# One more pair of the up projection as a seven-product step, and another rotation of PSUM banks beside it

## The chip, the core and the metric

One NeuronCore of a Trainium2 chip. TensorE (PE) multiplies, VectorE (DVE), ScalarE (ACT) and GpSimd (POOL) work on tiles, and DMAs are started from the queues of SyncE (SP), POOL and ACT. Each engine works through its own queue in order. The metric is the time of the whole kernel on the device in microseconds (us); lower is better.

## The reference

A residual block on x of 512 tokens by 1024 features, in float32. The change concerns the second half of it, the channel mixer:

```
h  = rms_norm(x, norm_ffn_g)
up = causal_dwconv(h @ w_up, conv_ffn_w)      # 1024 -> 2 * 2816, then 3 taps along the tokens
a, b = split(up, 2)
x  = x + (silu(a) * b) @ w_down               # 2816 -> 1024
```

Ahead of it stand a mixing layer (a gated short convolution and attention with forget gates) and behind it a last RMSNorm.

## The kernel before

**Layout and number format.** Features lie on partitions in blocks of 128, tokens along the free axis. Each float32 product is made of three matmuls: an operand is split into a rounded part ("h", as in `wh`, `x1h`, `gh`) and the rest ("l", as in `wl`, `x1l`, `gl`), and h·h, l·h and h·l are added up in PSUM. Weights come from DRAM in chunks (`raw_*`), in the order of the list `stream`. `split` makes a chunk's `wh` on ACT (L275) and its `wl` on DVE (L279, which needs `wh`). Two buffers each of `wh` and `wl` are used in turn, so a chunk can be split once PE has done with the chunk two places earlier.

**The up projection.** The 22 pairs j of 128 columns of a and of b are made in two phases, 0 to 11 and 12 to 21, and each phase is followed by down steps over what it made. There are two ways to make a pair:

- plain: two chunks of 1024 columns (`up12`, `up13` for pair 6), each summed over eight feature blocks in one PSUM bank (L309, and L327 for the first two blocks). Then DVE multiplies the bank by `rb2` into a tile `fz` (L1171), and three taps make `fu` (ACT L566, DVE L567 and L570).
- as a seven-product step (function `seven`): two by two blocks are multiplied with seven products in place of eight (Strassen-Winograd). A pair is two doubles, and each double comes as a chunk P of 768 and a chunk F of 1024 columns (`P18`, `F18`, `P19`, `F19`), multiplied at L327 into four banks at once, named `dn`. The function `merge` then puts the four banks together (ACT L1192; DVE L1193, L1197, L1201, L1202, L1206, and L1214 for `rb2`), and the same taps follow. The sums of weights that the F chunks need are made in DRAM by DMAs that add (`make_forms`: SP's L208, POOL's L211) while earlier stages run.

`SUP` names the pairs made in seven-product steps. Behind each pair `glu` applies SiLU on ACT (L1232) and multiplies a by b on POOL (`ge` L1235, `go` L1244). After each second pair, sums for the down steps (DVE L1253, L1254, L1257, L1258) and splits of the results (ACT L1262, DVE L1263, tile `gl`) follow.

**What sets the order.** PE runs the chunks in the order written. Work on ACT and DVE that need not be done at once goes into the list `later`, and `run_later` takes some of it after each split, up to an allowance in us:

```python
if any(("e",) in w[2] for w in later):
    run_later(k, {"u": 4.2, "P": 1.6, "F": 1.2}[nm[0]])
```

A merge puts nine items there. While one is waiting, the `fz` and the taps of the plain pairs behind it are queued up there too. Whoever takes a PSUM bank first calls `flush` with its number, which puts out all that stands in `later` up to the item that reads this bank. The plain pairs of phase 0 take their banks from the list `acc`, two a pair; seven-product steps take four, by `USETS`, in the order (products 2 and 3, products 4 and 5, products 1 and 6, product 7). The banks 6, 7, 0, 1 of pair 5 are so read at L1197, at L1202 and L1206, at L1192 and L1193, and at L1201. A scheduler then orders each engine's instructions; the tables below show the outcome.

Of the kernel before, what the change touches and what calls it, by code (L numbers as in the profile page):

```python
# [57 lines left out]
PLAIN = [(m, k) for m in (6, 7) for k in range(*PHASES[1])]  # L58
PCUTS = (0, 8, 12, 20)

SUP = ((1, 2, 5), (14, 17))
XF = (26, 0)
UPD = tuple(tuple(((j, q), (j, q + 1)) for j in js for q in (0, 2)) for js in SUP)
DOUBLES = GATES + UPD[0] + STEPS[0] + UPD[1] + STEPS[1]
# [6 lines left out]
def block_kernel(ctx, tc, xT, vecs, wv, win, wmix, wo, wup, wst, wdp, outT):  # L71
# [10 lines left out]
    def keep(ins):  # L82
        return tc.keep_in_program_order(ins)

    def bank(i, name):
        return ps.tile([P, S], F32, tag=f"b{i}", name=name)

    def ring(*ids):
        st = [0]

        def f(name):
            st[0] += 1
            return bank(ids[(st[0] - 1) % len(ids)], name)

        return f
# [33 lines left out]
    def step_chunks(n):  # L129
        m = len(DOUBLES[n])  # L130
        return [(f"P{n}", wst[n, :, : 3 * m * P], 3 * m * P), (f"F{n}", n, 4 * m * P)]
# [10 lines left out]
    for ph, (j0, j1) in enumerate(PHASES):  # L142
        for j in range(j0, j1):
            if j in SUP[ph]:
                stream += step_chunks(n) + step_chunks(n + 1)
# [72 lines left out]
    def slot():  # L218

        while todo_bg and todo_bg[0][0] <= make_forms.slot:  # L220
            todo_bg.pop(0)[1]()
        make_forms.slot += 1
# [14 lines left out]
    def flush(banks=None):  # L237

        def wanted(w):
            return set(w[2]) & set(banks) if banks is not None else True  # L240

        while any(map(wanted, later)):
            n = next(n for n, w in enumerate(later) if banks is None or wanted(w) or w[0] < len(parts))
            with after_split():
                later.pop(n)[3]()
# [501 lines left out]
    acc, bank_s, bank_t = ring(2, 0, 1), ring(3, 4), ring(5, 6)  # L747
# [76 lines left out]
    def seven(doubles, n0, sets, operand, done=None, of="q", tick=False):  # L824


        todo, wants = [], {}
        for n, d in enumerate(doubles):
            for kind in "PF":
                prods = []  # L830
                for s_, (i, q) in enumerate(d):
                    for f, g, b, h in PROD:
                        if (f < 3) == (kind == "P"):
                            wants.setdefault(f"{kind}{n0 + n}", []).append((of, q))
                            c = 3 * s_ + f if f < 3 else s_ + len(d) * (f - 3)
                            prods.append((c, i, operand(q, g), b, h))
                todo.append((f"{kind}{n0 + n}", prods))
        users = [{(i, b) for _, i, _, b, _ in prods} for _, prods in todo]
        for n, (name, prods) in enumerate(todo):
            if tick and name[0] == "P":  # L840
                slot()
            wh, wl = chunk(name)
            flush(wants[name])
            before = set().union(*users[:n])
            after = set().union(*users[n + 1 :])
            out = []
            for c, i, (xh, xl), b, h in prods:
                if i not in open_:
                    flush(sets[i])
                    open_[i] = [bank(x, f"dn{n0}{i}{x}") for x in sets[i]]  # L850
                cs = slice(c * P, (c + 1) * P)
                out.append((
                    open_[i][b][:, th[h]], (i, b), wh[:, cs], wl[:, cs], xh, xl,
                    (i, b) not in before, (i, b) not in after,
                ))
            passes(out, len(out))
            if name[0] == "F":
                for i in sorted({i for _, i, *_ in prods}):
                    if (i, 0) not in after:
                        done(i, open_.pop(i), sets[i])  # L860
            split_next()


    acc = ring(3, 4, 5, 6, 2, 7)
# [94 lines left out]
    for j in range(KB):  # L959
# [13 lines left out]
        else:  # L973
            if j == GJ:
                acc = ring(3, 4, 2, 7)
# [31 lines left out]
    acc = ring(0, 1, 5, 6, 3, 4, 2, 7)  # L1007
# [83 lines left out]
    def up_form(ph, q, g):  # L1091
        if g < 3:
            kb, hs = (2 * q, 2 * q + 1, 2 * q + 1)[g], th[(0, 0, 1)[g]]
            return x1h[:, kb, hs], x1l[:, kb, hs]
        n = XF[ph] + 4 * q + (0, 3, 1, 2)[g - 3]
        return gh[:, n, :], gl[:, n, :]
# [27 lines left out]
    def turns(*ids):  # L1124
        st = list(ids)

        def f(name):
            f.last = st.pop(0)
            flush((f.last,))
            return bank(f.last, name)  # L1130

        return f

    acc = turns(0, 1, *(2, 3, 4, 5) * 2, 6, 7, 0, 1, 2, 3, 4, 5)
    USETS = dict.fromkeys(SUP[1], (2, 3, 4, 5)) | {1: (2, 3, 4, 5), 2: (6, 7, 0, 1), 5: (6, 7, 0, 1)}
    ssq3 = xp.tile([P, S], F32, tag="ssq", name="ssq3")

    def place(ph, q):
# [2 lines left out]
    def up(j, ph, rb2, pu=None):  # L1141
# [6 lines left out]

        if j in SUP[ph]:
            c = 2 * SUP[ph].index(j)  # L1150
            slot()
            seven(
                UPD[ph][c : c + 2], NU[ph] + c, {j: USETS[j]}, lambda q, g: up_form(ph, q, g), of="x",
                done=lambda i, banks, ids: merge(ph, j, banks, ids, rb2, tap, uu),
# [27 lines left out]
    def merge(ph, j, banks, ids, rb2, tap, uu):  # L1182

        p23, p45, p16, p7 = banks[0], banks[1], banks[2], banks[3][:, th[0]]
        t, gs = {}, []

        def tile_of(nm):
            return fp.tile([P, S], F32, tag="fz", name=f"{nm}{j}", bufs=4)

        def z1():  # L1190
            t["z"] = tile_of("uz")
            nc.scalar.activation(t["z"][:, th[0]], p16[:, th[0]], AF.Copy)  # L1192
            nc.vector.tensor_add(t["z"][:, th[1]], p16[:, th[1]], t["z"][:, th[0]])  # L1193

        def m1():
            gs.append(tile_of("ua"))
            nc.vector.tensor_add(gs[0], p23, t["z"])  # L1197

        def u3():
            t["u"] = tile_of("uu")[:, : 2 * P]  # L1200
            nc.vector.tensor_add(t["u"], p7, t["z"][:, th[1]])  # L1201
            nc.vector.tensor_add(gs[0][:, th[1]], p45[:, th[1]], gs[0][:, th[1]])  # L1202

        def m2():
            gs.append(tile_of("ub"))
            nc.vector.tensor_add(  # L1206
                gs[1].rearrange(halves_of, h=2), p45.rearrange(halves_of, h=2),
                t["u"].unsqueeze(1).to_broadcast([P, 2, 2 * P]),
            )

        def fin(n):
            def f():
                g = gs[n]
                nc.vector.scalar_tensor_tensor(g, g, (1.0, -1.0)[n], rb2, op0=ALU.mult, op1=ALU.mult)  # L1214

            return f

        ev = ("e",)
        for f, us, x in (
            (z1, 0.42, 2), (m1, 0.7, 0), (u3, 0.85, 3), (m2, 0.7, 1),  # L1220
            (fin(0), 0.7, None), (lambda: tap(0, gs[0]), 1.4, None),
            (fin(1), 0.7, None), (lambda: tap(1, gs[1]), 1.4, None),
            (lambda: glu(ph, j, uu), 0, None),
        ):
            later.append((0, us, (ev,) if x is None else (ev, ids[x]), f))

    def glu(ph, j, uu):
# [11 lines left out]
        def sums():  # L1239
# [3 lines left out]
            def mul(eng):  # L1243
                return eng.tensor_mul(go[:, 0:2, :], a.rearrange(halves_of, h=2), b.rearrange(halves_of, h=2))  # L1244
            if j + 1 < PHASES[ph][1]:
                keep(mul(nc.vector if ph and j + 1 in SUP[ph] else nc.gpsimd))
            else:
# [80 lines left out]
    for ph, (j0, j1) in enumerate(PHASES):  # L1328
        if ph:
            acc = turns(*(6, 7, 0, 1) * 4)  # L1330
# [211 lines left out]
```

## Time and profile before

| | |
|---|---|
| median of 3 runs | 691.76 us (691.45 to 691.80) |
| the profiled execution, its own time | 692.09 us |
| its span, first to last instruction | 690.3 us |
| busy: PE, DVE, ACT, POOL | 682.4, 556.0, 368.5, 190.9 us |
| granted TensorE clock, mean | 0.997 |
| data moved by DMA | 137.54 MB |

The profile is one execution on the chip. Matmuls overlap: each has a row of about 0.28 us, and the next one starts 0.11 us later, so that their cost is read from the distance of their starts and not from their durations. On DVE and ACT, too, the next instruction starts somewhat ahead of the end that a row states.

### The profile page before, as it was taken

The page shows a single profiled execution, that of the slowest core. Times are in us where ns is not written, and L with a number is a line of the kernel's source. Part 1 is how long each engine was busy: PE and PEld are TensorE (multiplying, and loading weights), DVE is VectorE, ACT ScalarE, POOL GpSimd, SP SyncE. Part 2 cuts the span into 40 slices and gives each one's busy share as a digit, 9 for nine tenths or more (in the row PEclk, how much of TensorE's full clock was granted, in tenths as well). Part 3 has the DMA queues.
Part 4 walks back from the last instruction along what each step waited for, and adds up shares of the span by engine and source line. Part 5 has one row for each costly group of instructions (what it writes and reads, how often), then busy time and mean ns, then how long its engine had stood idle before and what let it go on. Part 6 is the DMA issues. An engine that isn't in the chain of part 4 may idle for free.

```text
span 690.3 us, 14714 instructions
## 1 busy us (share of the span) xinstructions
PE 682.4 (99%) x5936; PEld 681.1 (99%) x5936; DVE 556.0 (81%) x861; ACT 368.5 (53%) x581; POOL 190.9 (28%) x203
## 2 busy tenths in 40 slices
PE   9999999999999999999999999999999999999996
PEld 9999999999999999999999999999999999999995
DVE  6677887966578778868879699998786998998894
ACT  5575755555555444446554455546444555445672
POOL 6124946543021201213410144330100314332000
PEclk9999999999999999999999999999999999999998
DMA  8628999562577586788997498889945996776613
GB/s 309 221 62 287 216 239 219 124 138 88 166 168 204 165 263 203 231 311 213 162 309 232 126 241 233 179 240 257 248 150 172 296 265 166 172 186 167 186 31 123
DMA packets 66165, 137.54 MB, mean 199 GB/s; under 512 B 5888, under 2 KB 31760, under 8 KB 65840
## 3 DMA queue, kind: packets, MB, share of 16 engines
q1 hardware_dynamic: 45384, 107.28, 47.0%
q0 software_dynamic: 18896, 26.03, 24.4%
q10 hardware_dynamic: 1816, 3.29, 1.3%
q8 instruction: 46, 0.75, 0.4%
q14 instruction: 23, 0.19, 0.1%
HBM read 132.31 MB, written 47.71 MB: 261 GB/s over the span
## 4 chain that ended last, share of the span: by engine, by line
PE 99%; DVE 0%; DVEq 0%; issue 0%
PE dn L327 29%; PE p_up L309 21%; PE p_in L309 14%; PE p_up L327 6%; PE p_wo L309 6%; PE yc L309 3%; PE ya L309 3%; PE pa L477 2%; PE pb L479 2%; PE p_q L309 2%; PE p_k L309 2%; PE o L658 2%; PE tp L641 1%; PE pdB L309 1%; PE pdA L309 1%; PE s L612 1%
## 5 line engine op out<-in xcount | busy, mean ns | idle before, releaser
L211 POOL DMA_DIRECT2D f<-in_wst_dram x69 | 79.6, 1350 | 26.7 <-DMA f<-f 26.4
L309 PE MATMUL p_up<-x1h,wh_up 128*128 128x256 f32 x416 | 81.1, 276 | 0.0
L309 PE MATMUL p_up<-x1l,wh_up 128*128 128x256 f32 x416 | 81.0, 276 | 0.0
L309 PE MATMUL p_up<-x1h,wl_up 128*128 128x256 f32 x416 | 80.9, 276 | 0.0
L279 DVE TENSOR_TENSOR wl_F<-raw_F,wh_F 128x1024 fp32r<-128x1024 f32 (+1 forms) x43 | 56.1, 1304 | 19.0 <-ACT wh_F L275 18.9
L275 ACT ACTIVATE wh_F<-raw_F 128x1024 fp32r<-128x1024 f32 (+1 forms) x43 | 44.5, 1034 | 39.9 <-PE dn L327 26.4
L309 PEld LDWEIGHTS p_up<-x1h,wh_up 128*128 128x128 f32 x416 | 62.7, 188 | 0.0
L309 PEld LDWEIGHTS p_up<-x1l,wh_up 128*128 128x128 f32 x416 | 62.6, 188 | 0.0
L309 PEld LDWEIGHTS p_up<-x1h,wl_up 128*128 128x128 f32 x416 | 62.6, 188 | 0.0
L309 PE MATMUL p_in<-xgh,wh_in 128*128 128x256 f32 x288 | 56.8, 279 | 0.0
L309 PE MATMUL p_in<-xgh,wl_in 128*128 128x256 f32 x288 | 56.6, 278 | 0.0
L309 PE MATMUL p_in<-xgl,wh_in 128*128 128x256 f32 x288 | 56.5, 278 | 0.0
L1235 POOL TENSOR_TENSOR ge<-fu,fu 128x512 f32<-128x512 f32 x11 | 21.6, 1968 | 124.1 <-DVE fu L570 94.0
L279 DVE TENSOR_TENSOR wl_P<-raw_P,wh_P 128x768 fp32r<-128x768 f32 (+1 forms) x43 | 42.2, 981 | 14.5 <-ACT wh_P L275 8.7
L275 ACT ACTIVATE wh_P<-raw_P 128x768 fp32r<-128x768 f32 (+1 forms) x43 | 35.3, 820 | 33.5 <-PE dn L327 23.1
L327 PE MATMUL dn<-gl,wh_F 128*128 128x256 f32 x216 | 51.0, 276 | 0.0
L327 PE MATMUL dn<-gh,wh_F 128*128 128x256 f32 x216 | 51.0, 276 | 0.0
L279 DVE TENSOR_TENSOR wl_up<-raw_up,wh_up 128x1024 fp32r<-128x1024 f32 x34 | 45.2, 1328 | 6.3 <-ACT wh_up L275 6.3
L275 ACT ACTIVATE wh_up<-raw_up 128x1024 fp32r<-128x1024 f32 x34 | 35.9, 1055 | 20.7 <-PE p_up L309 10.1
L309 PEld LDWEIGHTS p_in<-xgh,wh_in 128*128 128x128 f32 x288 | 44.7, 188 | 0.7
L309 PEld LDWEIGHTS p_in<-xgl,wh_in 128*128 128x128 f32 x288 | 43.7, 188 | 0.0
L309 PEld LDWEIGHTS p_in<-xgh,wl_in 128*128 128x128 f32 x288 | 43.6, 188 | 0.0
(343 smaller groups left out, 2212.1 us busy)
## 6 DMA issues: line engine op xcount, KB each, us to landing
raw_F<-f SPq DMA_DIRECT2D x40, 512.0 KB, 5.5
raw_up<-in_wup_dram SPq DMA_DIRECT2D x34, 512.0 KB, 5.5
raw_P<-in_wst_dram SPq DMA_DIRECT2D x40, 384.0 KB, 5.7
raw_in<-in_win_dram SPq DMA_DIRECT2D x24, 512.0 KB, 3.8
f<-in_wst_dram POOLq DMA_DIRECT2D x41, 256.0 KB, 7.4
f<-in_wst_dram SPq DMA_DIRECT2D x19, 512.0 KB, 7.2
f<-in_wst_dram POOLq DMA_DIRECT2D x19, 512.0 KB, 8.4
f<-f SPq DMA_DIRECT2D x38, 256.0 KB, 6.0
```

Source lines behind the costliest of these rows:

```text
L211: return lambda: keep(nc.gpsimd.dma_start(dst, src, accum_op=ALU.add))
L275: ins = nc.scalar.activation(hi, raw, AF.Copy)
L279: ins = nc.vector.tensor_sub(lo, raw, hi.bitcast(F32))
L309: keep(nc.tensor.matmul(out[:, cs], w, x[:, cs], start=start and i == 0 and c == 0, stop=stop and i == 2 and c == len(cut) - 1,))
L327: keep(nc.tensor.matmul(out, wl if x == 1 else wh, xl if x == 2 else xh, start=opens and bk not in seen, stop=closes and bk not in left,))
L477: keep(nc.tensor.matmul(pa[t][:, :VW], xt, w[:, VB:], start=start, stop=stop))
L479: keep(nc.tensor.matmul(pb[t], xt, w[:, :VB], start=start and t % 2 == 0, stop=stop and t % 2 == 1))
L612: keep(nc.tensor.matmul(s[:, :nn], QT[pr][:, e, qs], KA[pr][:, e, :nn], start=True, stop=False))
L641: keep(nc.tensor.transpose(tp[:, ks], pt[:, ks], ident))
L658: keep(nc.tensor.matmul(o[:, 2 * P * e + c0 : 2 * P * (e + 1)], w, x[:, kb, c0:], start=e == 0 and kb == 0 and i == 0, stop=e == 1 and kb ...
L1235: keep(nc.gpsimd.tensor_mul(ge, a.rearrange(halves_of, h=2), b.rearrange(halves_of, h=2)))
```

## The change

Pair 6 is made in a seven-product step: the chunks `up12` and `up13` give way to `P18`, `F18`, `P19`, `F19`. Later steps get new numbers, so that the first down step's chunks are `P18`, `F18` before and `P20`, `F20` now. Three DMAs that start the sums of weights on SP and three that add to them on POOL come on top in the mixing stage, and the DMAs of the following sums stand at other places in those two queues.

```diff
-SUP = ((1, 2, 5), (14, 17))
+SUP = ((1, 2, 5, 6), (14, 17))
...
-    acc = turns(0, 1, *(2, 3, 4, 5) * 2, 6, 7, 0, 1, 2, 3, 4, 5)
-    USETS = dict.fromkeys(SUP[1], (2, 3, 4, 5)) | {1: (2, 3, 4, 5), 2: (6, 7, 0, 1), 5: (6, 7, 0, 1)}
+    acc = turns(0, 1, 2, 3, 4, 5, *(6, 7, 0, 1), 6, 7, 2, 3, 4, 5)
+    USETS = dict.fromkeys(SUP[1], (2, 3, 4, 5)) | {1: (2, 3, 4, 5), 2: (6, 7, 0, 1), 5: (6, 7, 0, 1), 6: (2, 3, 4, 5)}
```

The banks by pair of phase 0, from pair 5 on:

| pair | 5 | 6 | 7 | 8 | 9 | 10 | 11 |
|---|---|---|---|---|---|---|---|
| before | 6 7 0 1 | 2 3 | 4 5 | 6 7 | 0 1 | 2 3 | 4 5 |
| now | 6 7 0 1 | 2 3 4 5 | 6 7 | 0 1 | 6 7 | 2 3 | 4 5 |

First place: PE at the end of a seven-product step, with the semaphores that each instruction waits for. Before, behind pair 5 (`F17` is its last chunk) comes the plain pair 6:

```order
L327 MATMUL dn1657_5201<-gh_3988,wl_F17_5281 128x256
L327 MATMUL dn1650_5202<-gh_3988,wl_F17_5281 128x256
L327 MATMUL dn1651_5203<-gh_3988,wl_F17_5281 128x256
L327 MATMUL p_up12_5333<-x1h_3990,wh_up12_5310 128x256 [waits Activation_49]
L327 MATMUL p_up12_5333<-x1l_3991,wh_up12_5310 128x256
```

Now pair 6 ends with `F19`, and the plain pair 7 follows:

```order
L327 MATMUL dn1863_5345<-gh_3995,wl_F19_5425 128x256
L327 MATMUL dn1864_5346<-gh_3995,wl_F19_5425 128x256
L327 MATMUL dn1865_5347<-gh_3995,wl_F19_5425 128x256
L327 MATMUL p_up14_5480<-x1h_3997,wh_up14_5454 128x256 [waits DVE_49,Activation_49]
L327 MATMUL p_up14_5480<-x1l_3998,wh_up14_5454 128x256
```

The first matmul of the plain pair, which waited for ACT alone (its `wh`), now waits for DVE too.

Second place: DVE around the reading of pair 5's bank 6 (L1197, `ua5`). Before, this is in the plain pair 6, and the bank is next written by pair 8:

```order
L1171 TENSOR_TENSOR fz41_5327<-p_up9_5139,rb_n2_4668 128x512
L567 SCALAR_TENSOR_TENSOR fu40_5323<-fz40_5321,vec_64,fu40_5323 128x511
L279 TENSOR_TENSOR wl_up13_5387<-raw_up13_5190,wh_up13_5386 128x1024
L570 SCALAR_TENSOR_TENSOR fu40_5323<-fz40_5321,vec_64,fu40_5323 128x510
L567 SCALAR_TENSOR_TENSOR fu41_5390<-fz41_5327,vec_64,fu41_5390 128x511
L1193 TENSOR_TENSOR uz5_5397<-dn1650_5202,uz5_5397 128x256
L570 SCALAR_TENSOR_TENSOR fu41_5390<-fz41_5327,vec_64,fu41_5390 128x510
L1197 TENSOR_TENSOR ua5_5400<-dn1656_5200,uz5_5397 128x512
L1201 TENSOR_TENSOR uu5_5402<-dn1651_5203,uz5_5397 128x256
```

Now it stands behind the last chunk of pair 6, `wl_F19`, and the first of pair 7, `wl_up14`; pair 7 writes this bank:

```order
L279 TENSOR_TENSOR wl_F19_5425<-raw_F19_5201,wh_F19_5424 128x1024
L1258 SCALAR_TENSOR_TENSOR go1_5330<-go1_5330 128x256
L1263 TENSOR_TENSOR gl_3996<-ge1_5144,gh_3995 128x256
L279 TENSOR_TENSOR wl_up14_5455<-raw_up14_5233,wh_up14_5454 128x1024
L1263 TENSOR_TENSOR gl_3996<-go1_5330,gh_3995 128x512 x3
L567 SCALAR_TENSOR_TENSOR fu41_5464<-fz41_5342,vec_64,fu41_5464 128x511
L1193 TENSOR_TENSOR uz5_5471<-dn1650_5213,uz5_5471 128x256
L570 SCALAR_TENSOR_TENSOR fu41_5464<-fz41_5342,vec_64,fu41_5464 128x510
L1197 TENSOR_TENSOR ua5_5478<-dn1656_5211,uz5_5471 128x512
L279 TENSOR_TENSOR wl_up15_5534<-raw_up15_5289,wh_up15_5533 128x1024
```

The row L1197 moved past all the splits of pair 6 and past three rows L1263 of the pairs 2 and 3.

Third place: DVE at the end of phase 0, from the second chunk of the first down step to the third. Before:

```order
L1171 TENSOR_TENSOR fz111_6184<-p_up23_6115,rb_n2_4668 128x512
L279 TENSOR_TENSOR wl_F18_6179<-raw_F18_5953,wh_F18_6178 128x1024
L1263 TENSOR_TENSOR gl_3989<-go4_5972,gh_3988 128x512
L567 SCALAR_TENSOR_TENSOR fu111_6186<-fz111_6184,vec_64,fu111_6186 128x511
L1263 TENSOR_TENSOR gl_3989<-go4_5972,gh_3988 128x512
L570 SCALAR_TENSOR_TENSOR fu111_6186<-fz111_6184,vec_64,fu111_6186 128x510
L279 TENSOR_TENSOR wl_P19_6246<-raw_P19_6026,wh_P19_6245 128x768
```

Now, between `wl_F20` and `wl_P21`. The first four rows behind `wl_F20` (L1253, L1254, then L1171 for `fz101` and for `fz110`) are left out:

```order
L1171 TENSOR_TENSOR fz111_6193<-p_up23_6109,rb_n2_4675 128x512
L567 SCALAR_TENSOR_TENSOR fu101_6180<-fz101_6178,vec_64,fu101_6180 128x511
L1257 SCALAR_TENSOR_TENSOR go4_6105<-go4_6105 128x256
L570 SCALAR_TENSOR_TENSOR fu101_6180<-fz101_6178,vec_64,fu101_6180 128x510
L567 SCALAR_TENSOR_TENSOR fu110_6189<-fz110_6187,vec_64,fu110_6189 128x511
L1258 SCALAR_TENSOR_TENSOR go4_6105<-go4_6105 128x256
L570 SCALAR_TENSOR_TENSOR fu110_6189<-fz110_6187,vec_64,fu110_6189 128x510
L567 SCALAR_TENSOR_TENSOR fu111_6195<-fz111_6193,vec_64,fu111_6195 128x511
L1263 TENSOR_TENSOR gl_3996<-ge4_5962,gh_3995 128x256
L570 SCALAR_TENSOR_TENSOR fu111_6195<-fz111_6193,vec_64,fu111_6195 128x510
L1263 TENSOR_TENSOR gl_3996<-go4_6105,gh_3995 128x512 x3
L279 TENSOR_TENSOR wl_P21_6263<-raw_P21_6016,wh_P21_6262 128x768
```

Before, four instructions stand between the splits of the two chunks; now seventeen do, among them all six taps on DVE of the last three blocks.

## The prediction, made before the changed kernel had run

> **What bounds the kernel now.** I read the page first: the busy shares, then the chain that ended last.
>
> ```profile
> PE 682.4 (99%) x5936; PEld 681.1 (99%) x5936; DVE 556.0 (81%) x861; ACT 368.5 (53%) x581; POOL 190.9 (28%) x203
> PE 99%; DVE 0%; DVEq 0%; issue 0%
> ```
>
> PE is the chain, so a matmul less is time less, as long as nothing makes PE wait. Matmuls overlap, so I take their price from PE's timeline, at the first matmuls of pairs 2, 3, 4, 5, 6, 7 and 8:
>
> ```profile
> 360.16 0.28 PE L327 MATMUL dn<-x1h,wh_P 128*128 128x256 f32 x1
> ...
> 369.68 0.28 PE L327 MATMUL p_up<-x1h,wh_up 128*128 128x256 f32 x1
> ...
> 380.56 0.28 PE L327 MATMUL p_up<-x1h,wh_up 128*128 128x256 f32 x1
> ...
> 391.44 0.28 PE L327 MATMUL dn<-x1h,wh_P 128*128 128x256 f32 x1
> ...
> 400.96 0.28 PE L327 MATMUL p_up<-x1h,wh_up 128*128 128x256 f32 x1
> ...
> 411.84 0.28 PE L327 MATMUL p_up<-x1h,wh_up 128*128 128x256 f32 x1
> ...
> 422.72 0.28 PE L327 MATMUL p_up<-x1h,wh_up 128*128 128x256 f32 x1
> ```
>
> A seven-product pair (2, 5) takes 9.52 us for 4 x 7 x 3 = 84 matmuls, a plain one (3, 4, 6, 7) 10.88 us for 96: 0.1133 us each. Next I asked how busy DVE is around the change, by stretches (pair 6; the rest of phase 0; the first down steps; columns: PE, weight load, DVE, ACT, POOL):
>
> ```profile
> 401.10:412.00 10.90, 10.90 (x99) 10.90 (x98) 10.90 (x19) 3.68 (x6) 7.78 (x7) 1.00 1.00 225
> 412.00:466.20 54.20, 54.20 (x481) 54.20 (x480) 52.26 (x75) 28.59 (x43) 19.84 (x16) 1.00 0.87 216
> 466.20:473.40 7.20, 7.17 (x63) 6.97 (x63) 7.20 (x10) 5.86 (x8) 0.28 (x1) 1.00 1.02 237
> ```
>
> DVE is as full as PE here, though only 81% over the span. It hides behind PE with almost no room left, so the order in its queue decides.
>
> **The change part by part.** *Matmuls.* 96 become 84: 12 x 0.1133 = 1.36 us less on PE.
>
> *Splits and merge.* By rows below, DVE's starts lie 1.14 us (1024 columns) and 0.87 us (768) apart for a split, 0.60 for an `fz` or a 512-wide `gl`, 0.66 for a tap, 0.33 for a 256-wide row. Pair 6 then needs 2 x 0.87 + 2 x 1.14 = 4.0 us of splits in place of 2.3, and a merge of 4 x 0.60 + 3 x 0.33 = 3.4 us in place of two `fz` (1.2): 3.9 us more of DVE, in 1.36 us less of PE's time. What that costs depends on the two places where PE waits for a row behind it.
>
> *First wait: bank 6.* Pair 7 now writes the bank of pair 5 that L1197 reads. DVE and POOL before, from pair 5's last split on:
>
> ```profile
> 396.60 1.22 DVE L279 TENSOR_TENSOR wl_F<-raw_F,wh_F 128x1024 fp32r<-128x1024 f32 x1 [0.31 <-ACT wh_F L275]
> 397.74 0.68 DVE L1171 TENSOR_TENSOR fz<-p_up,rb_n 128x512 f32<-128x512 f32 x1
> ...
> 400.00 0.75 DVE L567 SCALAR_TENSOR_TENSOR fu<-fz,vec,fu 128x511 f32<-128x511 f32 x1
> 400.66 0.69 DVE L1171 TENSOR_TENSOR fz<-p_up,rb_n 128x512 f32<-128x512 f32 x1
> 401.26 0.74 DVE L570 SCALAR_TENSOR_TENSOR fu<-fz,vec,fu 128x510 f32<-128x510 f32 x1
> ...
> 402.52 1.50 DVE L567 SCALAR_TENSOR_TENSOR fu<-fz,vec,fu 128x511 f32<-128x511 f32 x1
> ...
> 406.39 0.41 DVE L1193 TENSOR_TENSOR uz<-dn,uz 128x256 f32<-128x256 f32 x1
> 406.72 0.74 DVE L570 SCALAR_TENSOR_TENSOR fu<-fz,vec,fu 128x510 f32<-128x510 f32 x1
> 407.38 0.68 DVE L1197 TENSOR_TENSOR ua<-dn,uz 128x512 f32<-128x512 f32 x1
> 402.17 1.29 POOL L1244 TENSOR_TENSOR go<-fu,fu 128x512 f32<-128x512 f32 x1 [13.74 <-ACT fu L566]
> ```
>
> Before, L1197 ends at 408.06, and its bank is next written by pair 8 at 422.72: 14.7 us of room. Now I add up DVE's queue from the same point, 396.60. Splits that replace the old ones: `wl_F17` 1.14, `wl_P18` 0.87 with about 0.3 us for its `wh`, `wl_F18` 1.14, `wl_P19` 0.87, `wl_F19` 1.14, `wl_up14` 1.14: 6.6 us. The other rows up to L1197: three `fz` 1.8, six taps 4.0, six 256-wide rows 2.0, three `gl` 1.8, L1197's own 0.68: 10.3 us. With 0.1 us for a second short wait for ACT, ahead of `wl_up14`, the bank is free at 396.60 + 6.6 + 10.3 + 0.1 = 413.6. PE wants it at 400.96 + 9.52 = 410.48. The wait is 3.1 us. The row at 402.52 took 1.50 us where its like takes 0.74 or 0.75, while POOL's multiply ran: 0.76 us more where such a meeting falls into the stretch. One does, as `go` of pairs 2 and 3 comes within it. I take 3.1 + 0.8 = 3.9 us, with ends of 2.9 and 4.6.
>
> [...]
>
> *A smaller wait: pair 9's bank 6*, read by pair 7's first `fz`. That row stands behind `wl_up18`, which starts only when PE is done with `up16` and ACT has made `wh` (about 1.2 us). Then 1.14 + 4 x 0.33 + 2 x 0.66 and the row's own 0.68: 5.7 to 5.9 us after `up16`, and PE gets there after one chunk, 5.44 us. I take 0.5 us (0 to 1.2).
>
> *Second wait: the third chunk of the down steps.* The end of phase 0 before, PE, DVE and ACT:
>
> ```profile
> 466.24 0.28 PE L327 MATMUL dn<-gh,wh_P 128*128 128x256 f32 x1
> ...
> 472.25 0.28 PE L327 MATMUL dn<-gl,wh_P 128*128 128x256 f32 x1
> 472.56 0.97 PE L327 MATMUL dn<-gh,wl_P 128*128 128x256 f32 x6
> 467.90 1.22 DVE L279 TENSOR_TENSOR wl_F<-raw_F,wh_F 128x1024 fp32r<-128x1024 f32 x1
> 469.03 0.68 DVE L1263 TENSOR_TENSOR gl<-go,gh 128x512 fp32r<-128x512 f32 x1
> 469.63 0.75 DVE L567 SCALAR_TENSOR_TENSOR fu<-fz,vec,fu 128x511 f32<-128x511 f32 x1
> ...
> 471.55 0.95 DVE L279 TENSOR_TENSOR wl_P<-raw_P,wh_P 128x768 fp32r<-128x768 f32 x1
> 472.42 1.22 DVE L279 TENSOR_TENSOR wl_F<-raw_F,wh_F 128x1024 fp32r<-128x1024 f32 x1
> 466.49 1.06 ACT L275 ACTIVATE wh_F<-raw_F 128x1024 fp32r<-128x1024 f32 x1 [0.95 <-ACT gh L1262]
> ```
>
> There is no room here even before: PE comes to `wl` of the third chunk at 472.36, the split ends at 472.50, and the matmuls behind it are 0.2 us late (0.31 from row to row in place of 0.11). Let T be the end of the last up chunk. PE needs that split 18 + 24 + 12 matmuls later, at T + 6.1. `wl_F20` starts at about T + 1.2, since its `wh` must wait for PE at T, and takes 1.14. Behind it now stand 4 x 0.33 (L1253, L1254, L1257, L1258), 3 x 0.60 (`fz`), 6 x 0.66 (taps), 0.33 + 3 x 0.60 (`gl`): 9.2 us. Then the split itself, 0.95: T + 12.5. In between, ACT must do its part of the taps behind a `wh` and a `gh`, and `ge`'s multiply may meet a row: 0.2 to 1.6 us, I take 0.9. The wait is 12.5 + 0.9 - 6.1 = 7.3 us, with ends of 6.0 and 8.2. The 0.2 us of before go into it. That PE comes later to T changes nothing, for the queue hangs on T.
>
> *The clock after a long wait.* The granted clock at the end of the span, and PE's first work:
>
> ```profile
> 682.91 0.61 PE L363 MATMUL pb_n<-ident,rc_n 128*128 128x128 f32 x4
> 686.00:686.50 0.50, 0.00 (x0) 0.00 (x0) 0.10 (x1) 0.00 (x0) 0.00 (x0) 0.84 1.09 381
> 686.50:687.00 0.50, 0.00 (x0) 0.00 (x0) 0.00 (x0) 0.00 (x0) 0.00 (x0) 0.50 1.07 375
> 1.05 4.21 PE L115 MATMUL warm<-ones 128*128 128x128 f32 x18 [1.05 <-DVE ones L107]
> 6.37 0.63 PE L479 MATMUL pb<-wh_v,xgh 128*128 128x256 f32 x2
> 6.79 0.55 PE L477 MATMUL pa<-wl_v,xgh 128*128 128x264 f32 x2
> 7.41 0.40 PE L477 MATMUL pa<-wl_v,xgh 128*128 128x264 f32 x2
> ```
>
> PE ended at 683.5, and 0.84 in the stretch from 686.0 puts the fall to 0.50 at about 686.3: 2.8 us idle were enough. At the start two matmuls took 0.42 us (6.37 to 6.79), and from 7 us on half as long: some 6 us of work from 1.05 ran slow, which loses 3.0. A wait of 7.3 us should meet both. I take 2.5 us (0 to 3.4) behind the second wait. Behind the first wait the clock may fall too or not, at the same price; I count none there.
>
> [...]
>
> *Queues.* POOL's added DMAs are of this kind:
>
> ```profile
> L211 POOL DMA_DIRECT2D f<-in_wst_dram x69 | 79.6, 1350 | 26.7 <-DMA f<-f 26.4 <-issue 0.2
> ```
>
> Three more cost POOL 3 x 1.35 = 4.1 us, and they and SP's three stand in the mixing stage, where only the up projection, far later, waits for what they make; in the up projection POOL is busy for 19.84 of 54.2 us, which hides those that changed places. The chunks of pair 6 are 2 x 768 + 2 x 1024 columns, 1.84 MB, in place of 1.05 MB, and SP loads up to four buffers of each kind ahead. I price all that at nothing; without that cover it is a late load, a rival below.
>
> *The sum.* -1.36 + 3.9 + 0.5 + 7.3 - 0.2 + 2.5 = +12.6 us. On the profiled execution's 692.09 us that gives 704.7; on the median of the runs, 691.76, which lies 0.33 lower, 704.4.
>
> **The rivals.** *The covers hold (not slower).* If ACT and DVE reached both rows in time, 1.36 and 0.2 us would be saved: 690.2. For it: PE never waits in the up projection before, and counted over the whole phase DVE has time left. It decides where the queue is shorter by 3.9 us ahead of L1197 and by 7.3 us ahead of `wl_P21`. Against it: the queue is in order and its rows have measured prices. 5%.
>
> *One wait only.* The first wait vanishes (the bank is read early enough) and the tail stays: 691.76 - 1.6 + 7.3 + 2.5 = 700.0; or the tail vanishes: 691.76 - 1.6 + 4.4 = 694.6. 6%.
>
> *The clock holds.* Both waits, no slow matmuls: 701.9. For it: the fall at the end was seen once, with no work waiting. 16%.
>
> *Loads come late.* DMA's share is 1.00 in pair 6 before; 0.79 MB more at that row's 225 GB/s is 3.5 us. If `F18` or `F19` landed late by that, or the first wait's clock fell for its full price as well, the time would be 707 to 709. Against it: no PE wait there before, and buffers filled chunks ahead. 8% beyond the range.
>
> **How the numbers follow.** The forecast, 704.4, has 65%, with its own range of 702.5 to 708 from the ends of the terms and the first wait's clock. The range adds the case of the held clock and its lower end: 700.3 to 708.3, which holds about 65 + 16 = 81%. A measurement of this kernel can tell about 0.2% (1.4 us) from no change. The rival at 690.2 is 0.23% faster, on the edge of that: 3% faster and 2% the same; all other cases are slower, 95%.
>
> **What would show it.** Right: pair 6's 84 matmuls in 9.5 us; PE idle for 3 to 4.6 us ahead of pair 7's first `p_up`, ended by DVE's `ua` (L1197); PE idle for 6 to 8 us between `wh` and `wl` of the third down chunk, ended by L279; a granted clock below 1.00 in the 7 us behind that. Wrong: no gap at one of the two places; a gap ended by a DMA; a PE gap in pair 6 itself.

## The result and the profile after

The changed kernel takes 706.75 us (median of 4 runs, 705.84 to 707.78), the kernel before 691.78 (691.45 to 691.94): a ratio of 1.0218, 95% interval 1.0202 to 1.0234, 15.0 us slower. The prediction was 704.4, with 700.3 to 708.3 as its range. The profiled execution is the longest of the four, 707.78 us with a span of 706.0.

From the page of the changed kernel: busy shares with instructions, the granted clock in 40 slices, and the chain that ended last.

```profile
PE 686.2 (97%) x5924; PEld 684.1 (97%) x5924; DVE 559.0 (79%) x868; ACT 369.9 (52%) x584; POOL 193.4 (27%) x206
PEclk9999999999999999999999989997999999999999
PE 30%; DVE 1%; DVEq 0%; issue 0%
```

PE has 12 matmuls fewer (5924 against 5936) and is busy for 3.8 us longer: some of its work ran at a lower clock. The clock row has two dips that the kernel before did not have, and the chain, which was PE alone over 99% of the span, is now followed back for 31% only: it reaches the second of the waits below, and DVE's split there. PE's waits, by what it waited for (sum, times, longest):

```profile
PE dn L327 <- DVE wl_P L279: 7.8, 1, 7.8
PE p_up L327 <- DVE ua L1197: 3.6, 1, 3.6
PE p_up L327 <- DVE fz L1171: 0.4, 1, 0.4
```

These are the three places that the prediction names. PE's timeline, at the ends of pair 6, of pair 8, of the second down chunk's `wh` and of all PE work; the bracket is the part of the idle time that the profile puts down to a releaser:

```profile
410.26 0.50 PE L327 MATMUL dn<-gh,wl_F 128*128 128x256 f32 x3
414.33 0.55 PE L327 MATMUL p_up<-x1h,wh_up 128*128 128x256 f32 x1 [3.56 <-DVE ua L1197]
...
438.76 0.39 PE L309 MATMUL p_up<-x1l,wh_up 128*128 128x256 f32 x2
439.52 0.36 PE L327 MATMUL p_up<-x1h,wh_up 128*128 128x256 f32 x1 [0.38 <-DVE fz L1171]
...
472.37 0.28 PE L327 MATMUL dn<-gh,wh_P 128*128 128x256 f32 x1
...
478.38 0.28 PE L327 MATMUL dn<-gl,wh_P 128*128 128x256 f32 x1
486.45 1.65 PE L327 MATMUL dn<-gh,wl_P 128*128 128x256 f32 x6 [7.79 <-DVE wl_P L279]
...
699.38 0.61 PE L363 MATMUL pb_n<-ident,rc_n 128*128 128x128 f32 x4
```

With 0.113 us from one matmul to the next, the next one was due at 410.60, 438.99 and 478.49. It came 3.73, 0.53 and 7.96 us late. The rows before that answer to them stand in the prediction: pair 7's first `p_up` at 411.84, the first down chunk at 466.24, the third's `wl` at 472.56 and the last matmul at 682.91. So the shift grows from +2.5 us at pair 7 to +6.1 at the first down chunk, +13.9 behind the second wait and +16.5 at the end of PE's work. The first step is a wait less the 12 matmuls, and the third is a wait. In the second PE waits 0.5 us and in the fourth not at all, and it loses 3.6 and 2.6 us all the same. The windows behind the two long waits show why (columns: PE, weight load, DVE, ACT, POOL, then the granted clock, DMA share, GB/s):

```profile
410.50:413.90 3.40, 0.26 (x3) 0.07 (x1) 3.40 (x7) 1.87 (x4) 0.17 (x1) 0.94 1.04 304
413.90:417.00 3.10, 2.67 (x12) 2.70 (x13) 3.10 (x5) 0.00 (x0) 3.10 (x5) 0.50 0.91 284
417.00:420.50 3.50, 3.50 (x19) 3.50 (x18) 2.44 (x4) 0.72 (x1) 2.19 (x3) 0.53 0.90 155
420.50:424.00 3.50, 3.50 (x33) 3.50 (x32) 0.00 (x0) 1.08 (x2) 0.00 (x0) 1.00 1.19 234
...
479.00:486.00 7.00, 0.00 (x0) 0.00 (x0) 6.75 (x11) 1.83 (x4) 4.05 (x3) 0.70 0.45 60
486.50:489.50 3.00, 3.00 (x14) 3.00 (x15) 2.34 (x3) 0.82 (x1) 0.00 (x0) 0.50 0.55 158
489.50:493.00 3.50, 3.50 (x22) 3.50 (x22) 0.43 (x2) 1.06 (x1) 0.00 (x0) 0.64 0.74 248
```

In 3.5 us PE does 33 matmuls at full clock and 19 at 0.53. From the shares, the clock was at half from about 413.5 to 420.3 (6.8 us) and from 481.8 to 492.0 (10.2 us). In the second stretch PE was still waiting for the first half of it.

In all, the last matmul ends 16.5 us later; the execution as a whole was 15.7 longer (707.78 against 692.09), because what follows the last matmul's start was 0.8 us shorter than in the profiled execution before (706.0 - 699.38 = 6.6 against 690.3 - 682.91 = 7.4).

### The profile page after: what moved, and what is told of

Same layout as the page of the kernel before. It is cut to its first block, busy times and chain, and to the rows that moved or that the text cites. A ratio compares the mean times of both kernels' runs of the same rounds, so it can differ in the third digit from the quotient of the medians.

```text
span 706.0 us, 14721 instructions
## 1 busy us (share of the span) xinstructions
PE 686.2 (97%) x5924; PEld 684.1 (97%) x5924; DVE 559.0 (79%) x868; ACT 369.9 (52%) x584; POOL 193.4 (27%) x206
## 5 line engine op out<-in xcount | busy, mean ns | idle before, releaser
L309 PE MATMUL p_up<-x1h,wh_up 128*128 128x256 f32 x392 | 77.2, 278 | 0.0
L309 PE MATMUL p_up<-x1h,wl_up 128*128 128x256 f32 x392 | 77.0, 278 | 0.0
L309 PE MATMUL p_up<-x1l,wh_up 128*128 128x256 f32 x392 | 76.8, 278 | 0.0
L309 PEld LDWEIGHTS p_up<-x1h,wh_up 128*128 128x128 f32 x392 | 59.8, 190 | 0.0
L309 PEld LDWEIGHTS p_up<-x1l,wh_up 128*128 128x128 f32 x392 | 59.5, 189 | 0.0
L279 DVE TENSOR_TENSOR wl_P<-raw_P,wh_P 128x768 fp32r<-128x768 f32 (+1 forms) x45 | 44.0, 978 | 15.7 <-ACT wh_P L275 9.3
L327 PE MATMUL dn<-gl,wh_F 128*128 128x256 f32 x228 | 55.4, 281 | 0.0
L327 PE MATMUL dn<-gh,wh_F 128*128 128x256 f32 x228 | 55.4, 281 | 0.0
L279 DVE TENSOR_TENSOR wl_up<-raw_up,wh_up 128x1024 fp32r<-128x1024 f32 x32 | 41.9, 1308 | 13.4 <-ACT wh_up L275 13.3
L327 PEld LDWEIGHTS dn<-gh,wh_F 128*128 128x128 f32 x228 | 43.9, 193 | 0.0
L327 PEld LDWEIGHTS dn<-gl,wh_F 128*128 128x128 f32 x228 | 43.9, 193 | 0.0
```

The lines of the kernel that those rows point to most:

```text
L279: ins = nc.vector.tensor_sub(lo, raw, hi.bitcast(F32))
L309: keep(nc.tensor.matmul(out[:, cs], w, x[:, cs], start=start and i == 0 and c == 0, stop=stop and i == 2 and c == len(cut) - 1,))
L327: keep(nc.tensor.matmul(out, wl if x == 1 else wh, xl if x == 2 else xh, start=opens and bk not in seen, stop=closes and bk not in left,))
```

## Experiments

The theory: the order of DVE's queue makes the two long waits, each wait halves the clock behind it, and nothing else in the change costs time. The rivals: the new order of PSUM banks costs by itself; a fourth seven-product step costs by itself, by its loads and splits, wherever it stands; the slow stretches cost nothing, since PE would have met DVE's delay later anyway.

**The banks alone.** The kernel before, pair 6 plain, with the banks turned so that pairs 6 and 7 take the banks that they have in the changed kernel:

```diff
-    acc = turns(0, 1, *(2, 3, 4, 5) * 2, 6, 7, 0, 1, 2, 3, 4, 5)
+    acc = turns(0, 1, 2, 3, 4, 5, 2, 3, 6, 7, 0, 1, 6, 7, 2, 3, 4, 5)
```

> The kernel before, with plain pair 6, and the new rotation alone: pair 7 on banks 6 and 7, pair 8 on 0 and 1, pair 9 on 6 and 7. Theory (PE waits because VectorE comes late to L1197): before, L1197 ends at 408.06 and pair 7 starts at 411.84, so the bank is free 3.8 us early; 691.8 us, the same as before within 0.2%, and no wait of PE at pair 7. Rival (the rotation itself costs: fewer turns between uses of a bank): PE waits at pair 7 or 9 and the time is 693 us or more.

691.76 us against 692.06, a ratio of 0.9996 (0.9987 to 1.0005), and no wait of PE in the phase. The banks cost only together with a DVE queue that reads them late.

**Another bank for pair 7.** The changed kernel, with pair 7 starting on bank 0, which L1193 reads two rows earlier than L1197 reads bank 6:

```diff
-    acc = turns(0, 1, 2, 3, 4, 5, *(6, 7, 0, 1), 6, 7, 2, 3, 4, 5)
+    acc = turns(0, 1, 2, 3, 4, 5, 0, 1, 6, 7, 0, 1, 2, 3, 4, 5)
```

> The changed kernel, with pair 7 on banks 0 and 1, pair 8 on 6 and 7, pair 9 on 0 and 1. Pair 5's bank 0 is read at L1193, which ends about 1.3 us ahead of L1197 (412.92 against 414.18). Theory: the first wait is shorter by 1.0 to 1.3 us, so about 2.5 us, and ends with L1193. If a wait of 2.5 us lets the clock hold, 3 us more are saved: 702.5 us; if not, 705.5 us. Rival (PE waits for something that pair 7 needs in any case, its split or its load): the wait stays at 3.7 us and the time at 706.7 us.

703.94 us, a ratio of 1.0177 (1.0163 to 1.0192). From PE's timeline, and from the windows behind it (the clock is the third column from the end):

```profile
410.39 0.50 PE L327 MATMUL dn<-gh,wl_F 128*128 128x256 f32 x3
413.04 0.38 PE L327 MATMUL p_up<-x1h,wh_up 128*128 128x256 f32 x1 [2.15 <-DVE uz L1193]
```

```profile
413.50:417.50 4.00, 4.00 (x25) 4.00 (x24) 3.74 (x7) 0.00 (x0) 3.71 (x4) 0.63 0.92 317
417.50:421.00 3.50, 3.50 (x31) 3.50 (x30) 0.00 (x0) 0.54 (x1) 2.62 (x3) 0.93 0.91 137
```

PE was due at 410.73, so the wait is 2.3 us in place of 3.7, and it now ends with L1193: the wait belongs to whichever row reads the bank. PE's waits for `fz` grew from 0.4 us to 1.5 in two places, which takes back most of the 1.4. What is left of the 2.8 us gained is clock: in the profiled execution (706.09, the longest of its four) the slow stretch was about 3.4 us in place of 6.8, and the other three, 703.7 to 704.0, had a higher mean clock, 0.993 against 0.988. The time lies between the two that were expected (702.5 and 705.5).

**Fewer rows in the tail.** The changed kernel without DVE's two taps of pair 11's blocks (four rows between `wl_F20` and `wl_P21`):

```diff
-            taps(u, z, CF + 3 * (2 * j + i))
+            if j == 11:
+                nc.scalar.activation(u, z, AF.Copy, scale=col(CF + 3 * (2 * j + i) + 2))
+            else:
+                taps(u, z, CF + 3 * (2 * j + i))
```

> The changed kernel without VectorE's four tap instructions of pair 11 (L567 and L570, twice): the output then lacks two of three taps for that pair. All four stand in VectorE's queue between the splits of the second and third chunk of the down steps. Theory (that queue is the second wait): 4 x 0.66 = 2.6 us less wait there, and a little more where those taps wait for ScalarE or meet GpSimd; 8.0 becomes 4.5 to 5.4 us, the time 703.3 to 704.2 us, with the clock falling as before. Rival (the wait hangs on a load or on PSUM): wait and time unchanged, 706.7 us.

702.83 us, a ratio of 1.0155 (1.0141 to 1.0169). PE's timeline at the third down chunk:

```profile
481.84 0.58 PE L327 MATMUL dn<-gh,wl_P 128*128 128x256 f32 x1 [4.88 <-DVE wl_P L279]
```

The second wait is shorter by 2.9 us (7.79 to 4.88 by the bracket), what four taps of 0.66 and their wait for ACT (0.24) come to. The time fell by 3.9, to half a us below the range expected: the slow stretches of this execution are about 3.4 and 6.8 us long, in place of 6.8 and 10.2, so about 1 us more came from the clock. The rows that the prediction counted ahead of `wl_P21` are the wait.

**Work in the second wait.** The changed kernel with 60 extra matmuls, into a bank of their own, between `wh` and `wl` of chunk `P21`:

```diff
-    def passes(prods, lead):
+    def passes(prods, lead, busy=0):
...
+            if x == 1 and busy:
+                idle = bank(5, "busy")[:, : 2 * P]
+                for n in range(busy):
+                    keep(nc.tensor.matmul(idle, gh[:, n % 14, :P], gl[:, n % 14, :], start=True, stop=True))
+                busy = 0
...
-            passes(out, len(out))
+            passes(out, len(out), 60 if name == "P21" else 0)
```

> The changed kernel with 60 more matmuls (6.8 us of PE, into a bank that is free then) in the place of the second wait, ahead of the matmuls that need the late split. Theory (PE is idle there and the clock falls for the idleness): the split ends when it did, PE is idle for about 1 us in place of 8, the granted clock stays at 1.00 behind it, and the time falls by the 2.5 to 3 us that slow matmuls cost: 703.7 to 704.3 us. Rival (the slow matmuls behind the wait have another cause, or none of the time is theirs): 706.7 us or, if PE was not really free, up to 713 us.

704.05 us, a ratio of 1.0176 (1.0163 to 1.0190): with 60 matmuls more it is 2.7 us faster. The windows, behind the first wait and from the end of the second:

```profile
413.50:417.00 3.50, 3.19 (x15) 3.22 (x16) 3.50 (x6) 0.00 (x0) 3.50 (x5) 0.55 0.63 181
417.00:421.00 4.00, 4.00 (x36) 4.00 (x36) 1.92 (x3) 0.72 (x1) 1.68 (x2) 0.96 0.98 204
484.00:495.00 11.00, 10.37 (x92) 10.24 (x91) 8.80 (x13) 5.05 (x7) 0.00 (x0) 1.00 0.73 218
```

The clock stays at 1.00 behind the second wait, and it is still low behind the first, where nothing was added. There the slow stretch is about 3.4 us long in this execution, in place of 6.8, so the 2.7 us are not the second wait's alone.

**Work in both waits.** The same, and 33 repeats of the last matmul of pair 6 ahead of pair 7:

```diff
...
+        for _ in range(more):
+            keep(nc.tensor.matmul(out, wl, xh, start=False, stop=_ == more - 1))
...
-            passes(out, len(out), 60 if name == "P21" else 0)
+            passes(out, len(out), 60 if name == "P21" else 0, 33 if name == "F19" else 0)
```

> The changed kernel with extra matmuls in both long waits: 33 repeats of the last matmul of pair 6 ahead of the first wait (what they add to that bank is the part of the result that this kernel changes), and the 60 of the run with extra matmuls ahead of the second. They fill time in which PE waits anyway. If the clock behind the first wait costs about 3.1 us as the slow stretch of 6.8 us in the changed kernel's trace says: 704.05 - 3.1 = 701.0 us (700.3 to 702), near the 701.9 that the prediction gives for waits without slow matmuls, and clock 1.00 behind both. If the slow matmuls there cost nothing, because PE would have waited for DVE later anyway: 704 (703.5 to 704.5).

702.43 us, a ratio of 1.0148 (1.0133 to 1.0163). From PE's timeline, and from the windows behind both waits:

```profile
410.62 3.90 PE L338 MATMUL dn<-gh,wl_F 128*128 128x256 f32 x33
414.36 0.28 PE L332 MATMUL p_up<-x1h,wh_up 128*128 128x256 f32 x1
...
469.52 0.28 PE L332 MATMUL dn<-gh,wh_P 128*128 128x256 f32 x1
...
483.63 0.97 PE L332 MATMUL dn<-gh,wl_P 128*128 128x256 f32 x6 [0.63 <-DVE wl_P L279]
...
693.99 0.61 PE L370 MATMUL pb_n<-ident,rc_n 128*128 128x128 f32 x4
```

```profile
414.40:421.00 6.60, 6.60 (x61) 6.60 (x60) 4.80 (x7) 1.67 (x2) 4.77 (x5) 1.00 0.81 181
483.70:494.00 10.30, 10.30 (x91) 10.30 (x92) 8.11 (x12) 5.13 (x7) 0.00 (x0) 1.00 0.70 219
```

Pair 7 starts at 414.36 here and at 414.33 in the changed kernel, and both wait 0.4 us for the same `fz` later, so the two differ behind it in the clock alone. From there to the first down chunk it is 55.16 us here and 58.04 there: the slow stretch behind the first wait cost 2.9 us. From the second wait's end to the last matmul it is 210.36 and 212.93: 2.6 us. The profiled executions differ by 5.4 us (707.78 and 702.41). The median fell by 4.3 only, since in two of the four runs of the changed kernel (705.84 and 705.99, mean clock 0.988 against 0.986) less was slow than in the profiled one. The run came out 1.4 us above the 701.0 expected of it, and above its range: against the run with work in the second wait alone it gained 1.6, because there the slow stretch behind the first wait was only 3.4 us long. The third rival falls; 702.43 lies close to the 701.9 that the prediction gave for waits with no slow matmuls.

**Pair 7 in place of pair 6.** A plain pair now stands between the last two steps:

```diff
-SUP = ((1, 2, 5, 6), (14, 17))
+SUP = ((1, 2, 5, 7), (14, 17))
...
-    acc = turns(0, 1, 2, 3, 4, 5, *(6, 7, 0, 1), 6, 7, 2, 3, 4, 5)
+    acc = turns(0, 1, 2, 3, 4, 5, 2, 3, 4, 5, 2, 3, 4, 5, 2, 3)
...
```

> Pair 7 takes the seven-product step in place of pair 6, so that a plain pair with two banks of its own stands between pairs 5 and 7 as one stands between 2 and 5; the tail after the last up chunk is as in the changed kernel. If the order of DVE's queue makes the two waits and each wait brings its own loss of clock: the wait ahead of the first p_up of the next pair is gone with the slow clock behind it, 706.75 - 3.7 - 3.1 = 700.0 us (699 to 701), and the wait at the third down chunk stays at 7 to 8 us. If a fourth seven-product step costs as such (its loads, its splits, wherever it stands): 705 to 707, with a first wait somewhere else.

700.94 us, a ratio of 1.0128 (1.0112 to 1.0144). The windows where the first wait was, and PE's timeline in the tail:

```profile
404.00:416.00 12.00, 12.00 (x108) 12.00 (x107) 10.48 (x19) 5.06 (x9) 4.66 (x5) 1.00 0.94 202
416.00:424.00 8.00, 8.00 (x73) 8.00 (x73) 7.28 (x10) 4.61 (x6) 0.00 (x0) 1.00 0.89 258
```

```profile
479.93 1.44 PE L327 MATMUL dn<-gh,wl_P 128*128 128x256 f32 x5 [7.79 <-DVE wl_P L279]
```

The first wait and its clock are gone and the second wait is as long as it was, with the same matmuls, chunks and bytes. So the fourth step as such does not cost the time; its place does. PE's wait for an `fz` grew from 0.4 to 0.8 us, which explains part of the 0.9 that it lies above the 700.0.

**More time for deferred rows.** Behind each split the kernel runs deferred DVE rows up to a budget; for an up chunk's split it is 4.2 us:

```diff
-            run_later(k, {"u": 4.2, "P": 1.6, "F": 1.2}[nm[0]])
+            run_later(k, {"u": 5.0, "P": 1.6, "F": 1.2}[nm[0]])
```

> The changed kernel with one number other: the time that is set aside for deferred work behind each split of an up chunk is 5.0 us in place of 4.2, so that DVE gets through its deferred rows earlier. Same matmuls, same chunks, same loads, same banks. If both waits are only a matter of what stands ahead in DVE's queue: the wait at the third down chunk is gone (its rows have been run by then) with its clock, 706.75 - 8.0 - 2.8 = 696.0, and the first wait shrinks by about 1.5 us to 2.2 us: 694.5 with the clock loss behind it as now, 693.1 if it is one short stretch of slow clock, 691.4 if the clock holds: 691.4 to 694.5. If the loads or the count of DVE's work in the phase set the end: 703 or more.

694.10 us, a ratio of 1.0030 (1.0016 to 1.0044). Both waits are gone. One of 3.1 us stands elsewhere, in pair 10, and not at pair 7 where I had expected what was left; PE's timeline there, and the windows behind it:

```profile
443.45 0.28 PE L327 MATMUL p_up<-x1l,wh_up 128*128 128x256 f32 x1
446.67 0.51 PE L327 MATMUL p_up<-x1h,wl_up 128*128 128x256 f32 x2 [2.94 <-DVE wl_up L279]
```

```profile
446.00:447.50 1.50, 0.83 (x7) 0.83 (x8) 1.50 (x3) 0.19 (x1) 0.00 (x0) 1.00 0.00 0
447.50:451.00 3.50, 3.50 (x21) 3.50 (x20) 2.50 (x4) 0.53 (x1) 0.85 (x1) 0.57 0.90 282
451.00:455.00 4.00, 4.00 (x35) 4.00 (x35) 2.61 (x5) 1.82 (x3) 2.48 (x3) 0.95 0.96 260
```

12.7 us less by one number: the change's cost lies in the order, not in the amount of work. But a larger budget also puts rows ahead of a split that PE then needs. The same number in the kernel before shows that alone:

> The kernel before with the one number alone: 5.0 us in place of 4.2 set aside for deferred rows behind an up chunk's split. If the gain of the version with pairs 1, 2, 4 and 6 comes from the 12 matmuls less, and the number only keeps its queue in order: no gain here. With three seven-product pairs the larger number puts rows ahead of a split that PE then waits for, once, for about 2 us, and one stretch of 3.4 us at half clock behind it costs 1.7: 692.0 + 2 = 694.0, or 695.7 with the clock (693.5 to 696). If the number itself is what gains: 690 to 691.3.

694.94 us, a ratio of 1.0046 (1.0031 to 1.0061), with this wait in pair 8, on PE's timeline:

```profile
425.75 0.51 PE L327 MATMUL p_up<-x1h,wl_up 128*128 128x256 f32 x2 [2.49 <-DVE wl_up L279]
```

**Pairs 1, 2, 4 and 6.** A plain pair stands ahead of the third step and of the fourth, and the third comes one pair earlier:

```diff
-SUP = ((1, 2, 5, 6), (14, 17))
+SUP = ((1, 2, 4, 6), (14, 17))
```

with the banks of the run with pair 7, first with the budget left at 4.2 us:

> Pairs 1, 2, 4 and 6 in seven-product steps with the number left at 4.2 us. If the distance between the steps removes the first wait and part of the second (a plain pair more lies behind the last step, so fewer of its deferred rows are left at the end of the phase): waits of about 0.8 us at a p_up and 2 us at the third down chunk, 690.4 + 2.8 = 693.2, with 1.7 for one stretch of half clock 694.9 (692.8 to 695.5). If the number 5.0 alone removed the second wait: it stays at 7 to 8 us here, 700 us.

693.30 us, a ratio of 1.0026 (1.0016 to 1.0036). PE's wait in the tail is down to 2.2 us, and in the up projection only one of 0.5 us for an `fz` is left. The expectation had the reason wrong: as many plain pairs lie behind the last step as in the changed kernel (7 to 11), so what is left over at the end must be less because pair 4's rows are deferred a pair earlier than pair 5's; that was not tried by itself. PE's timeline in the tail:

```profile
473.91 0.86 PE L327 MATMUL dn<-gh,wl_P 128*128 128x256 f32 x5 [2.04 <-DVE wl_P L279]
```

Then with the budget of 5.0 us as well:

> Pairs 1, 2, 4 and 6 take the seven-product step (a plain pair between 2, 4 and 6), with the time set aside of 5.0 us. As many matmuls as the changed kernel has, 12 fewer than the kernel before. If nothing but the two waits and their clock made the change slow: no wait over 0.6 us, clock at 1.00 through the phase, 691.8 - 1.36 - 0.2 + 0.6 = 690.8 us (690.2 to 691.6), a ratio of 0.998 to 1.000 to the kernel before. If DVE is too full for a fourth step anywhere, waits of 2 us or more turn up in the phase: 694 or more.

690.84 us (11 runs, 690.28 to 692.04) against 691.97, a ratio of 0.9981 (0.9972 to 0.9990). The longest waits of PE in the phase and the first down steps:

```profile
PE dn L327 <- DVE wl_P L279: 0.3, 1, 0.3
PE p_up L327 <- DVE wl_up L279: 0.2, 1, 0.2
```

The busy shares on its page:

```profile
PE 681.5 (99%) x5924; PEld 679.9 (99%) x5924; DVE 557.7 (81%) x868; ACT 370.7 (54%) x584; POOL 193.5 (28%) x206
```

This is what 12 matmuls less are worth when DVE keeps up: 1.1 us at the medians, of the 1.4 that they take off PE. No stretch of the phase is left at a lower clock, since no wait is left. The medians in one table (us):

| seven-product pairs of phase 0 | budget 4.2 | budget 5.0 |
|---|---|---|
| 1, 2, 5 (before) | 691.8 | 694.9 |
| 1, 2, 5, 6 (changed) | 706.8 | 694.1 |
| 1, 2, 4, 6 | 693.3 | 690.8 |

## Why the prediction was nearly right, and where it was short

By its own terms, against the profiled execution:

| term | predicted | measured |
|---|---|---|
| 12 matmuls less | -1.4 | -1.3 (pair 6 from 400.98 to 410.60, 9.62 us; before 10.88) |
| first wait, bank 6 | 3.9 (2.9 to 4.6) | 3.73 |
| clock behind it | 0 | 2.9 |
| pair 9's bank 6 | 0.5 | 0.53 |
| second wait, less before's own 0.2 | 7.1 (5.8 to 8.0) | 7.76 |
| clock behind it | 2.5 (0 to 3.4) | 2.6 |

The measured terms add up to 16.2 of the 16.5 us by which the last matmul came later. No run shows the term of 2.5 us for the clock, or its upper end of 3.4, as the price of a wait: both were estimates, beside the 3.0 us that the prediction read from the start of the span. The runs showed 2.6 us behind the second wait and 2.9 behind the first.

The first matmul of pair 6 on PE's timeline, and on DVE's and POOL's the rows up to the one that frees the bank:

```profile
400.98 0.36 PE L327 MATMUL dn<-x1h,wh_P 128*128 128x256 f32 x1
396.57 1.23 DVE L279 TENSOR_TENSOR wl_F<-raw_F,wh_F 128x1024 fp32r<-128x1024 f32 x1 [0.30 <-ACT wh_F L275]
...
402.01 1.49 DVE L567 SCALAR_TENSOR_TENSOR fu<-fz,vec,fu 128x511 f32<-128x511 f32 x1
...
413.50 0.68 DVE L1197 TENSOR_TENSOR ua<-dn,uz 128x512 f32<-128x512 f32 x1
401.66 1.29 POOL L1244 TENSOR_TENSOR go<-fu,fu 128x512 f32<-128x512 f32 x1 [13.25 <-DVE fu L570]
```

The sum over the queue put the bank's release at 414.4 (413.6 and one meeting with POOL); L1197 ended at 414.18, and the meeting is there, 1.49 us at 402.01. From `wl_F17` to L1197 DVE is never idle for more than 0.3 us, nor from `wl_F20` to `wl_P21` in the tail: both waits are the length of its queue.

The step that failed is the sentence "Behind the first wait the clock may fall too or not, at the same price; I count none there." It fell, and cost 2.9 us in the profiled execution. The prediction had its own evidence against the zero: it read from the end of the span that 2.8 us idle were enough, and it forecast a wait of 3.9. Only the upper end of its range had this cost. By its own price of 2.5 us for that too, the forecast would have been 706.9 at the median, against 706.75; that it would have come so near is partly luck, for the second wait was 0.7 us longer than forecast and the end of the execution 0.8 shorter. More than half of the 0.7 is in these rows of DVE's and POOL's timelines:

```profile
479.98 1.75 DVE L570 SCALAR_TENSOR_TENSOR fu<-fz,vec,fu 128x510 f32<-128x510 f32 x1
481.97 0.75 DVE L567 SCALAR_TENSOR_TENSOR fu<-fz,vec,fu 128x511 f32<-128x511 f32 x1 [0.24 <-ACT fu L566]
479.21 1.97 POOL L1235 TENSOR_TENSOR ge<-fu,fu 128x512 f32<-128x512 f32 x1 [10.23 <-ACT gh L1262]
```

The tap beside `ge`'s multiply took 1.75 in place of 0.74, a meeting of 1.0 us, and ACT's tap behind it came 0.24 late. So the next row started 1.99 us behind this tap's start in place of 0.66: 1.3 in a range of 0.2 to 1.6, of which I had taken 0.9. Another 0.15 is `wl_F20`, which started 1.35 us behind T in place of 1.2, and the rest is small. Both taps that ran beside a multiply in these rows, at 402.01 and at 479.98, took longer than the others' 0.74: 1.49 and 1.75 us, and each ended 0.55 us behind POOL's row.

On the rivals: "the covers hold" needs both queues shorter, which only the pairs 1, 2, 4 and 6 with the larger budget bring (690.84; the rival said 690.2). "One wait only" is the run with pair 7 (700.94; the rival said 700.0). "The clock holds" is the run with work in both waits (702.43 against 701.9). "Loads come late" did not happen: every long wait ends with DVE. That the loads and the fourth step were free, as the prediction priced them, is shown by pair 7 in the place of pair 6 and by pairs 1, 2, 4 and 6, to within the 0.3 us that these last gained less than the matmuls saved.

## What to carry to other kernels

A saving on the engine that bounds the kernel is worth its price only where the engines behind it have room in that stretch: DVE was 81% busy over the span and full just there, and 1.4 us saved on PE cost 12 us of waits. To price a move, add up the in-order queue row by row from a known time to the row that PE waits for; three such sums here came out within 0.7 us. And reckon with half clock behind a shorter wait too, not only behind the longest: waits of 2.3 us (pair 7 on bank 0), 3.1 (the changed kernel with the larger budget) and 3.7 (the changed kernel) were followed by it, and one of 2.7 (the kernel before with the larger budget) was not. In the changed kernel half clock was a third of the loss, 5.5 of 16.5 us. Where a wait is left, the order of deferred work and the distance between heavy steps are cheaper to change than the work.

## What was not expected of the hardware

The half clock came in stretches of about 3.4, 6.8 and 10.2 us: 3.4 in the changed kernel with the larger budget (0.43 x 2 x 3.5 + 0.05 x 2 x 4.0), 6.8 and 10.2 in the changed one. It does not start a fixed time after PE goes idle: in the changed kernel it began 2.9 us after PE was out of matmuls at the first wait (410.6 to 413.5) and 3.3 us at the second (478.5 to 481.8), while with the larger budget PE resumed at 446.67 and the clock fell only at about 448. And a wait of 2.7 us in the kernel before with the larger budget left it at 1.00 in the profiled execution:

```profile
426.00:430.00 4.00, 4.00 (x37) 4.00 (x37) 3.09 (x5) 0.72 (x1) 0.77 (x1) 1.00 0.82 234
```

The record of the clock in the traces of the two kernels shows a grid. In the changed kernel, from the first change on, the changes lie 409.60, 6.83, 61.44, 10.24 and 211.63 us apart, which is 120, 2, 18, 3 and 62 stretches of 3.413 us; in the kernel before there are two, 679.25 us apart, which is 199. Laid out on this grid, these are the stretches at the waits of the changed kernel, with PE's busy time from the windows view. For pair 7 on bank 0 it is the 3.4 us ahead of the fall, which its windows put at about 414.5 (417.5 - 2 x 0.37 x 4.0):

| run | stretch | PE busy in it | clock in it | clock behind it |
|---|---|---|---|---|
| pair 7 on bank 0 | about 411.1 to 414.5 | 1.5 us | 1.00 | 0.50 |
| changed, first wait | 410.07 to 413.48 | 0.69 | 1.00 | 0.50 |
| changed, behind it | 413.48 to 416.90 | 2.57 | 0.50 | 0.50 |
| changed, second wait | 485.16 to 488.58 | 2.13 | 0.50 | 0.50 |
| changed, behind it | 488.58 to 491.99 | 3.41 | 0.50 | 1.00 |

In the traces of the two kernels, from the first change on, half clock followed the four stretches at full clock with 0.69 us of work or less (0.69, 0.33, 0.60 and 0.00), and none of those with 2.83 or more; none lies between. At both waits of the changed kernel the clock came back behind a stretch that was busy throughout (3.41 us). At the start of its span it came back behind one with 2.83 us of work (0.47 to 3.88). So a stretch need not be idle as a whole for half clock to follow. That a wait's place on this grid decides what it costs is an estimate from these cases: 2.7 us of waiting cost nothing at the clock in the execution above, 3.1 us brought one slow stretch of 3.4 us, which costs 1.7, and the first wait, 3.6 us by the bracket in three traces, brought a slow stretch of 6.8 us in the changed kernel (2.9 us lost) and of 3.4 in the runs with fewer taps and with work in the second wait. That this is also why one kernel's runs here lie 1.7 to 2.4 us apart (705.84 and 707.51; 703.70 and 706.09) fits, but one execution of each kernel has a trace, and no run moved a wait along the grid by itself.
